# Dense expert stage: weight loads of four experts, stored first products reloaded into the lower parts' buffers

## Chip, core and metric

The kernel runs on one core of a Trainium2 chip. The time is the device time of one execution in microseconds (us). Seven names recur: PE (TensorE, the matrix engine; PEld is its weight load), DVE (VectorE), ACT (ScalarE), POOL (GpSimd), SP (the engine that issues most DMA transfers), DMA (the 16 transfer engines of the core) and PSUM (the accumulation memory that PE writes).

## What is computed

A decoder block over 1024 tokens of width 1024: two attention branches, a memory attention, and then an expert layer with 16384 experts. The change touches the expert layer alone:

```python
def peer_ffn(h, w_q, sub_keys, u, v):
    ...
    best_s, pos = lax.top_k(cand_s, PEER_TOPK)
    best_i = jnp.take_along_axis(cand_i, pos, axis=-1)
    g = jax.nn.softmax(best_s, axis=-1)
    ...
        a = jnp.einsum('cd,ced->ce', hc, u[ic])
        a = jax.nn.gelu(a, approximate=False) * gc.astype(hc.dtype)
        return jnp.einsum('ce,ced->cd', a, v[ic])
```

Each token picks 8 x 16 experts; the output is the sum over them of gelu(h . u) times a gate weight times the row v.

## The kernel before

The eight blocks of 128 tokens are treated in two ways. Blocks 0 to 3 are *gathered*: `gathered_u` (L1027) and `gathered_v` (L1041) fetch one expert row per token with an indirect DMA from POOL, 128 rows per block and table, and DVE multiplies each row (L1038 for u, L1057 for v). Seven buffers `rows` hold the fetched rows. These steps are spread over the whole program by `Pace` (L44): each piece of PE work adds its time to a budget, and a row step is written out when the budget allows, so that the written order mixes them with whatever runs. A scheduler then sets the order on each engine from priorities and its own estimate of durations; what it has set is fixed, and every engine takes its instructions strictly in that order.

Blocks 4 to 7 are *dense* (`dense`, L1190): for them all 16384 experts are computed, in 128 slices of 128 experts, with gate weights that are zero where a token has not picked the expert. Below, "expert" e stands for such a slice. For each there is a first product (h times u, 24 matmuls of 512 columns: eight column parts, each in three products of higher and lower parts), GELU, a multiplication by the gate weights, and a second product with the slice's rows of v. The helper `split` (L111) cuts a float32 tile into a higher part (ACT, L112) and a lower part (DVE, L113) for the matmuls.

Before the gate weights are complete, the first products of experts 0 to 47 are computed, passed through GELU and stored in DRAM (`ga`, L1226). From 2215 us on the second products run in groups of G = 4 experts. `group(gi)` (L1239) makes the left operands, `second(gi, cs)` (L1258) splits the four value rows and runs eight output tiles of 12 matmuls; `group(gi + 1)` is written ahead of `second(gi)`. In groups 0 to 11 a first product is reloaded from `ga` into `c` (L1248); in groups 12 to 31 `first(e)` (L1208) computes it. The buffers that matter, and what frees each:

- `wl` (2 buffers): the gate weights of two experts, 512 KB, runs of 512 bytes in DRAM; multiplied in place with the first products (L1252) and free after the split.
- `c` (1 buffer): a reloaded first product, free after L1252.
- `c0`, `c1` (7 each): higher and lower part of an expert's left operand, free when all eight tiles of the group have used them, which is at the group's end. Two groups hold eight, so the last expert of the next group waits for the first of the running one.
- `vraw` (4): a raw value row block, free after the split into `v0`, `v1` (4 each), which are again free at a group's end.
- `uraw` (3), `uT0`, `uT1` (2 each): the same for the first product.

SP issues all loads but the gathers, in one queue; an instruction that waits there holds up all that follow it.

Of the kernel before, what the change touches and what calls it, by code (L numbers as in the profile page):

```python
# [9 lines left out]
F32 = mybir.dt.float32  # L10
F32R = mybir.dt.float32r
# [3 lines left out]
AF = mybir.ActivationFunctionType  # L15
# [5 lines left out]
P = 128  # L21
# [5 lines left out]
ND = NB - NG  # L27
DT = ND * P
# [56 lines left out]
class K:  # L85
# [941 lines left out]
    def gathered_u(self, b, r):  # L1027
        nc, a, ep = self.nc, self.a, self.ep
        ii = r["ii"]
        h3 = ep.tile([P, D], F32, name="h3s", bufs=1)  # L1030
        nc.sync.dma_start(h3, self.h3[b])
        aa = r["aa"] = ep.tile([P, P], F32, name="aa", bufs=3)
        for j in range(P):
            u = self.rows()
            nc.gpsimd.indirect_dma_start(out=u, out_offset=None, in_=a["peer_u"][0],  # L1035
                                         in_offset=bass.IndirectOffsetOnAxis(ap=ii[:, j:j + 1], axis=0))
            with self.tc.issue_after(self.last_dve):
                nc.vector.scalar_tensor_tensor(u, u, 1.0, h3, op0=OP.mult, op1=OP.mult, accum_out=aa[:, j:j + 1])  # L1038
            yield self.u_each

    def gathered_v(self, b, r):  # L1041

        nc, a, ep = self.nc, self.a, self.ep
        w = ep.tile([P, P], F32, name="wexp", bufs=1)
        nc.scalar.activation(w, r["aa"], AF.Gelu)
        nc.vector.tensor_tensor(w, w, r["gg"], op=OP.mult)
        o = ep.tile([P, D], F32, name="h3s", bufs=1)
        for j in range(P):
            with self.tc.high_priority(offset=V_AHEAD):
                v = self.rows()  # L1050
                nc.gpsimd.indirect_dma_start(out=v, out_offset=None, in_=a["peer_v"][0],  # L1051
                                             in_offset=bass.IndirectOffsetOnAxis(ap=r["ii"][:, j:j + 1], axis=0))
                with self.tc.issue_after(self.last_dve):
                    if j == 0:
                        nc.vector.tensor_scalar(o, v, w[:, :1], None, op0=OP.mult)
                    else:
                        nc.vector.scalar_tensor_tensor(o, v, w[:, j:j + 1], o, op0=OP.mult, op1=OP.add)  # L1057
            yield V_EACH or self.u_each
        self.finish(b, o, [self.rows() for _ in range(3)])
        yield 1.0  # L1060
# [129 lines left out]
    def dense(self, psum, early):  # L1190

        nc, a = self.nc, self.a
# [3 lines left out]
        with ExitStack() as ctx:  # L1196
# [11 lines left out]
            def first(e):  # L1208
                uT = load_u(e)
                o = self.acc()  # L1210
                for k in range(KD):
                    self.mm3(o, [u[:, k] for u in uT], [x[:, k] for x in h3], k == 0, k == KD - 1)
                self.pace.tick(KD * 3 * 0.216)
                return o
# [20 lines left out]
            sp = E(self.pool("sp"))  # L1235
            accu = sp.tile([P, ND, D], F32, name="accu")
            G = 4

            def group(gi):  # L1239
                cs = []  # L1240
                for e in range(gi * G, gi * G + G):
                    if e % 2 == 0:
                        w2 = sp.tile([P, 2 * ND, 2, P // 2], F32, name="wl", bufs=2)
                        nc.sync.dma_start(w2, self.Wd[:, :, e:e + 2].rearrange("j p e n -> p j e n"))
                    w = w2[:, :, e % 2]
                    if e in ga:
                        c = sp.tile([P, DT], F32, name="c", bufs=1)
                        nc.sync.dma_start(c, ga[e])  # L1248
                    else:
                        c = first(e)  # L1250
                        nc.scalar.activation(c, c, AF.Gelu)
                    nc.vector.tensor_tensor(w, c.rearrange("p (j n) -> p j n", j=2 * ND), w, op=OP.mult)  # L1252
                    ch = [sp.tile([P, DT], F32R, name=f"c{j}", bufs=7) for j in range(2)]
                    self.split(w, *[x.rearrange("p (j n) -> p j n", j=2 * ND) for x in ch])
                    cs.append(ch)
                return cs

            def second(gi, cs):  # L1258
# [7 lines left out]
                for i in range(ND):  # L1266
                    for d in range(2):
# [14 lines left out]
                        self.pace.tick(G * 3 * 0.216)  # L1282

            cs = group(0)
            for gi in range(NE // G):
                nx = group(gi + 1) if gi + 1 < NE // G else None
                second(gi, cs)
                cs = nx
# [102 lines left out]
WHOLE = {("P", 1), ("G", 1), ("M", 1)}  # L1391
PAIRS = {(2, 0)}
KEEP, A_BUFS, O_BUFS = 4, 2, 2
U_BUFS, V_BUFS = 3, (4, 4, 4)
SELECT_EACH = (5.0, 7.0)
U_EACH, ROUTE_EACH = (1.9, 1.8, 1.9, 1.3, 2.0), 3.0
ROUTE_LAG, EXPERT_LAG = 300, 3000
# [31 lines left out]
```

## Time and profile before

| What | Value |
|---|---|
| median of 3 runs | 3498.06 us (3488.26 to 3505.14) |
| the profiled execution | 3498.35 us |
| its span, first to last instruction | 3496.6 us, mean granted clock 0.93 |
| PE busy | 3027.1 us (87%) |
| DVE busy | 2851.4 us (82%) |
| ACT, POOL busy | 1399.1 us (40%), 1402.9 us (40%) |
| DMA | 964.64 MB, mean 276 GB/s |

The span lies within 2 us of the profiled execution's time, and that execution within 0.3 us of the median. Busy shares are means over stages with different limits: the second products, which the change touches, fill the last 1280 us.

### The profile page before, as it was taken

How to read it: one execution, taken by the hardware profiler on the slowest of the kernel's cores; microseconds unless marked ns; L12 is line 12 of the kernel's file. 1: busy time of each engine (PE TensorE's matmuls, PEld its weight loads, DVE VectorE, ACT ScalarE, POOL GpSimd, SP SyncE). 2: the span in 40 equal slices, each digit the busy share in tenths (PEclk: the TensorE clock that was granted, in tenths of full speed). 3: DMA queues.
4: the chain of work that ended last, by engine and by line, in shares of the span. 5: the costliest groups of instructions: out<-in, count | busy, mean ns of one | idle time of the engine just before them, and what ended most of it. 6: DMA issues, size and time to landing. Idle time of an engine off the chain costs nothing. (4 is left out here: it accounts for less than half of the span.)

```text
span 3496.6 us, 42268 instructions
## 1 busy us (share of the span) xinstructions
PE 3027.1 (87%) x13234; PEld 2292.2 (66%) x13234; DVE 2851.4 (82%) x6623; ACT 1399.1 (40%) x2537; POOL 1402.9 (40%) x1122
## 2 busy tenths in 40 slices
PE   8999888798788798777998896587899999999997
PEld 6778766553345675445676674466677888787886
DVE  6656554588968989887999888687799999899998
ACT  5756344245656441323546465222122222222222
POOL 0010000012245346653122665424457666776665
PEclk9999999899898899888999998799899999999999
DMA  4575443335789579887485999989899999999998
GB/s 139 163 187 136 168 136 137 128 121 187 215 285 303 145 263 359 305 322 281 141 294 210 372 366 345 381 305 326 304 349 373 384 381 371 359 365 384 377 380 285
DMA packets 394210, 964.64 MB, mean 276 GB/s; under 512 B 36713, under 2 KB 146049, under 8 KB 392577
## 3 DMA queue, kind: packets, MB, share of 16 engines
q0 software_dynamic: 155264, 560.01, 45.1%
q1 hardware_dynamic: 238720, 401.94, 33.5%
q8 instruction: 104, 1.70, 0.2%
q14 instruction: 122, 0.99, 0.1%
HBM read 871.64 MB, written 90.18 MB: 275 GB/s over the span
## 5 line engine op out<-in xcount | busy, mean ns | idle before, releaser
L1035 POOL DMA_INDIRECT rows<-in_peer_u_dram,ii x512 | 689.0, 1346 | 916.8 <-DVE rows L1038 365.5
L1051 POOL DMA_INDIRECT rows<-in_peer_v_dram,ii x512 | 649.6, 1269 | 425.4 <-DVE h3s L1057 290.3
L1057 DVE SCALAR_TENSOR_TENSOR h3s<-rows,wexp,h3s 128x1024 f32<-128x1024 f32 x508 | 651.0, 1282 | 36.3 <-DMA rows<-in_peer_v_dram,ii 27.4
L1038 DVE SCALAR_TENSOR_TENSOR rows<-rows,h3s 128x1024 f32<-128x1024 f32 x512 | 611.6, 1219 | 79.1 <-DMA rows<-in_peer_u_dram,ii 75.7
L135 PE MATMUL acc<-fT,uT 128*128 128x512 f32 x1024 | 415.1, 405 | 43.3 <-ACT uT L112 23.9
L137 PE MATMUL acc<-fT,uT 128*128 128x512 f32 x1024 | 412.3, 403 | 13.8 <-DVE uT L113 13.7
L136 PE MATMUL acc<-fT,uT 128*128 128x512 f32 x1024 | 409.6, 400 | 0.0
L112 ACT ACTIVATE c<-wl 128x512 fp32r<-128x512 f32 x128 | 80.1, 631 | 812.2 <-PE out L136 461.6
L149 POOL TENSOR_TENSOR rstd<-msq,mhalf 128x1 f32<-128x1 f32 (+1 forms) x42 | 35.3, 840 | 592.9 <-DVE msq L147 582.5
L135 PEld LDWEIGHTS acc<-fT,uT 128*128 128x128 f32 x1024 | 196.8, 192 | 88.7 <-ACT uT L112 24.8
L137 PEld LDWEIGHTS acc<-fT,uT 128*128 128x128 f32 x1024 | 196.7, 192 | 66.5 <-DVE uT L113 20.9
L136 PE MATMUL kept<-v,c 128*128 128x512 f32 x512 | 206.7, 406 | 34.5 <-DVE v L113 34.5
L135 PE MATMUL kept<-v,c 128*128 128x512 f32 x512 | 202.3, 401 | 37.8 <-ACT v L112 36.9
L112 ACT ACTIVATE uT<-uraw 128x1024 fp32r<-128x1024 f32 x128 | 135.5, 1059 | 246.8 <-PE acc L136 130.5
L136 PEld LDWEIGHTS acc<-fT,uT 128*128 128x128 f32 x1024 | 196.9, 192 | 38.7
L113 DVE TENSOR_TENSOR w<-wraw,w 128x512 fp32r<-128x512 f32 (+1 forms) x176 | 116.8, 680 | 118.6 <-ACT w L112 112.0
L135 PE MATMUL out<-v,c 128*128 128x512 f32 x512 | 204.1, 399 | 8.9 <-DVE accu L1281 8.9
L137 PE MATMUL kept<-v,c 128*128 128x512 f32 x512 | 203.9, 398 | 0.0
L136 PE MATMUL out<-v,c 128*128 128x512 f32 x512 | 202.9, 396 | 0.0
L137 PE MATMUL out<-v,c 128*128 128x512 f32 x512 | 202.6, 396 | 0.0
L568 ACT ACTIVATE junk<-W,xb 128x384 bf16<-128x384 f32 (+5 forms) x186 | 163.7, 880 | 75.7 <-DVE xb L566 55.2
L112 ACT ACTIVATE w<-wraw 128x512 fp32r<-128x512 f32 (+1 forms) x176 | 105.9, 619 | 186.5 <-PE acc L136 81.8
(361 smaller groups left out, 6780.8 us busy)
## 6 DMA issues: line engine op xcount, KB each, us to landing
uraw<-in_peer_ut_dram SPq DMA_DIRECT2D x128, 512.0 KB
vraw<-in_peer_v_dram SPq DMA_DIRECT2D x128, 512.0 KB
Wd<-wbuf SPq DMA_DIRECT2D x64, 512.0 KB
wl<-Wd SPq DMA_DIRECT2D x64, 512.0 KB
wraw<-in_w_in_dram SPq DMA_DIRECT2D x40, 512.0 KB
fraw<-in_w_in_dram SPq DMA_DIRECT2D x32, 512.0 KB
wraw<-in_w_out_dram SPq DMA_DIRECT2D x24, 512.0 KB
ga<-gelu SPq DMA_DIRECT2D x48, 256.0 KB
```

Of the source, the lines that this page charges most:

```text
L112: self.nc.scalar.activation(hi, src, AF.Copy)
L113: self.last_dve = self.nc.vector.tensor_tensor(lo, src, hi.bitcast(F32), op=OP.subtract).ins
L135: nc.tensor.matmul(out, l[0], r[0], start=start, stop=False)
L136: nc.tensor.matmul(out, l[0], r[1], start=False, stop=False)
L137: self.last_pe = nc.tensor.matmul(out, l[1], r[0], start=False, stop=stop).ins
L149: nc.gpsimd.tensor_tensor(r, v, self.mhalf[:, :n], op=OP.pow)
L568: nc.scalar.activation(junk[:, :(b + 1) * P], self.W[b], AF.Sign, bias=xb[:, j:j + 1].bitcast(F32), accum_out=s[:, j:j + 1])
L1035: nc.gpsimd.indirect_dma_start(out=u, out_offset=None, in_=a["peer_u"][0], in_offset=bass.IndirectOffsetOnAxis(ap=ii[:, j:j + 1], axis=0))
L1038: nc.vector.scalar_tensor_tensor(u, u, 1.0, h3, op0=OP.mult, op1=OP.mult, accum_out=aa[:, j:j + 1])
L1051: nc.gpsimd.indirect_dma_start(out=v, out_offset=None, in_=a["peer_v"][0], in_offset=bass.IndirectOffsetOnAxis(ap=r["ii"][:, j:j + 1], axi ...
L1057: nc.vector.scalar_tensor_tensor(o, v, w[:, j:j + 1], o, op0=OP.mult, op1=OP.add)
```

## The change

Four edits. The gate weights of a whole group are loaded in one transfer of 1 MB (`wg`, two buffers, runs of 1024 bytes) in place of two of 512 KB. A stored first product is reloaded into the `c1` buffer of its own expert, read there as plain float32, multiplied into the weights, and the buffer then takes the lower part; the single buffer `c` is gone. `vraw` has three buffers in place of four. For the gathered blocks, `aa` has two buffers in place of three, and GELU and gate multiplication work in it in place, without `wexp`.

```diff
--- before.py
+++ after.py
@@ -1029,7 +1029,7 @@
         ii = r["ii"]
         h3 = ep.tile([P, D], F32, name="h3s", bufs=1)
         nc.sync.dma_start(h3, self.h3[b])
-        aa = r["aa"] = ep.tile([P, P], F32, name="aa", bufs=3)
+        aa = r["aa"] = ep.tile([P, P], F32, name="aa", bufs=2)
         for j in range(P):
             u = self.rows()
             nc.gpsimd.indirect_dma_start(out=u, out_offset=None, in_=a["peer_u"][0],
@@ -1041,8 +1041,8 @@
     def gathered_v(self, b, r):
 
         nc, a, ep = self.nc, self.a, self.ep
-        w = ep.tile([P, P], F32, name="wexp", bufs=1)
-        nc.scalar.activation(w, r["aa"], AF.Gelu)
+        w = r["aa"]
+        nc.scalar.activation(w, w, AF.Gelu)
         nc.vector.tensor_tensor(w, w, r["gg"], op=OP.mult)
         o = ep.tile([P, D], F32, name="h3s", bufs=1)
         for j in range(P):
@@ -1239,18 +1239,19 @@
             def group(gi):
                 cs = []
                 for e in range(gi * G, gi * G + G):
-                    if e % 2 == 0:
-                        w2 = sp.tile([P, 2 * ND, 2, P // 2], F32, name="wl", bufs=2)
-                        nc.sync.dma_start(w2, self.Wd[:, :, e:e + 2].rearrange("j p e n -> p j e n"))
-                    w = w2[:, :, e % 2]
+                    if e % G == 0:
+                        wg = sp.tile([P, 2 * ND, G, P // 2], F32, name="wl", bufs=2)
+                        nc.sync.dma_start(wg, self.Wd[:, :, e:e + G].rearrange("j p e n -> p j e n"))
+                    w = wg[:, :, e % G]
+                    ch = [sp.tile([P, DT], F32R, name=f"c{j}", bufs=7) for j in range(2)]
                     if e in ga:
-                        c = sp.tile([P, DT], F32, name="c", bufs=1)
+
+                        c = ch[1].bitcast(F32)
                         nc.sync.dma_start(c, ga[e])
                     else:
                         c = first(e)
                         nc.scalar.activation(c, c, AF.Gelu)
                     nc.vector.tensor_tensor(w, c.rearrange("p (j n) -> p j n", j=2 * ND), w, op=OP.mult)
-                    ch = [sp.tile([P, DT], F32R, name=f"c{j}", bufs=7) for j in range(2)]
                     self.split(w, *[x.rearrange("p (j n) -> p j n", j=2 * ND) for x in ch])
                     cs.append(ch)
                 return cs
@@ -1391,7 +1392,7 @@
 WHOLE = {("P", 1), ("G", 1), ("M", 1)}
 PAIRS = {(2, 0)}
 KEEP, A_BUFS, O_BUFS = 4, 2, 2
-U_BUFS, V_BUFS = 3, (4, 4, 4)
+U_BUFS, V_BUFS = 3, (4, 4, 3)
 SELECT_EACH = (5.0, 7.0)
 U_EACH, ROUTE_EACH = (1.9, 1.8, 1.9, 1.3, 2.0), 3.0
 ROUTE_LAG, EXPERT_LAG = 300, 3000
```

No arithmetic is changed. On every engine the order is the same as before up to the first weight load of the second products. Three places from there on matter. In the listings a row is one instruction: line, operation, written tile, read tile, shape; numbers behind a name tell its instances apart. In brackets stand what it waits for: PE, DVE, Activation (ACT), or the lanes of earlier transfers (DMAHW).

The first is SP's queue in the stored groups. Before, in a stretch of about one group (`wl` weights, `vraw` raw values, `c` the reloaded product):

```order
L1244 DMA wl<-Wd 128x8x128 [waits DMAHW6_49,Activation_49]
L1263 DMA vraw<-in_peer_v_dram 128x1024 [waits DMAHW7_49,DVE_49]
L1248 DMA c<-ga_15442 128x512 [waits DMAHW5_49,DVE_49]
L1263 DMA vraw<-in_peer_v_dram 128x1024 [waits DMAHW1_49,Activation_49]
L1244 DMA wl<-Wd 128x8x128 [waits DVE_49]
L1248 DMA c<-ga_15523 128x512 [waits DMAHW0_49,DVE_49]
L1263 DMA vraw<-in_peer_v_dram 128x1024 [waits DMAHW4_49]
```

After, one whole group:

```order
L1250 DMA c_19131<-ga_14748 128x512 [waits DMAHW4_49,PE_49]
L1250 DMA c_19300<-ga_14865 128x512 [waits DMAHW5_49,PE_49]
L1250 DMA c_19306<-ga_14996 128x512 [waits DMAHW6_49,PE_49]
L1250 DMA c_19312<-ga_15087 128x512 [waits PE_49]
L1264 DMA vraw<-in_peer_v_dram 128x1024 [waits DMAHW0_49,DVE_49]
L1244 DMA wl<-Wd 128x8x256 [waits DMAHW1_49,DVE_49]
L1264 DMA vraw<-in_peer_v_dram 128x1024 [waits DMAHW2_49,DVE_49]
L1264 DMA vraw<-in_peer_v_dram 128x1024 [waits DMAHW3_49,DVE_49]
L1264 DMA vraw<-in_peer_v_dram 128x1024 [waits DMAHW0_49,DMAHW4_49,DVE_49,Activation_49]
```

The reloads, which waited for DVE (L1252) one at a time, now wait for PE, four together, and the value loads stand behind them.

The second is DVE at a stored group's handover (`c_` and `v_` lower parts, `wl` the product with the weights, `accu` the sum of an output tile). Before:

```order
L113 TENSOR_TENSOR c_19933<-wl,c_19932 128x512
L113 TENSOR_TENSOR v_20130<-vraw,v_20129 128x1024
L1281 TENSOR_TENSOR accu<-accu,out 128x512
L113 TENSOR_TENSOR c_20103<-wl,c_20102 128x512
L113 TENSOR_TENSOR c_20110<-wl,c_20109 128x512
L113 TENSOR_TENSOR v_20136<-vraw,v_20135 128x1024
L1252 TENSOR_TENSOR wl<-c,wl 128x8x64
L113 TENSOR_TENSOR v_20142<-vraw,v_20141 128x1024
L113 TENSOR_TENSOR c_20119<-wl,c_20118 128x512
L113 TENSOR_TENSOR v_20148<-vraw,v_20147 128x1024
```

After:

```order
L113 TENSOR_TENSOR v_20080<-vraw,v_20079 128x1024
L1254 TENSOR_TENSOR wl<-c_19887,wl 128x8x64
L1282 TENSOR_TENSOR accu<-accu,out 128x512
L1254 TENSOR_TENSOR wl<-c_20056,wl 128x8x64
L113 TENSOR_TENSOR c_19887<-wl,c_19886 128x512
L1254 TENSOR_TENSOR wl<-c_20062,wl 128x8x64
L113 TENSOR_TENSOR c_20056<-wl,c_20055 128x512
L1254 TENSOR_TENSOR wl<-c_20068,wl 128x8x64
L113 TENSOR_TENSOR c_20062<-wl,c_20061 128x512
L113 TENSOR_TENSOR v_20086<-vraw,v_20085 128x1024
L113 TENSOR_TENSOR c_20068<-wl,c_20067 128x512
L113 TENSOR_TENSOR v_20092<-vraw,v_20091 128x1024
```

All four products of reloaded experts now stand between the first value's lower part and the second's; before, one product stood among the values and the others among the rows that follow. About ten gathered rows follow in either.

The third is DVE at a live group's handover (`h3s` a gathered row, `uT` the lower part for a first product). Before:

```order
L113 TENSOR_TENSOR c_23631<-wl,c_23630 128x512
L113 TENSOR_TENSOR v_23992<-vraw,v_23991 128x1024
L1281 TENSOR_TENSOR accu<-accu,out 128x512
L113 TENSOR_TENSOR v_23998<-vraw,v_23997 128x1024
L113 TENSOR_TENSOR v_24004<-vraw,v_24003 128x1024
L113 TENSOR_TENSOR v_24010<-vraw,v_24009 128x1024
L1057 SCALAR_TENSOR_TENSOR h3s<-rows,wexp,h3s 128x1024 x2
L1252 TENSOR_TENSOR wl<-acc,wl 128x8x64
```

After:

```order
L113 TENSOR_TENSOR c_23498<-wl,c_23497 128x512
L1282 TENSOR_TENSOR accu<-accu,out 128x512
L113 TENSOR_TENSOR v_23899<-vraw,v_23898 128x1024
L113 TENSOR_TENSOR v_23905<-vraw,v_23904 128x1024
L113 TENSOR_TENSOR v_23911<-vraw,v_23910 128x1024
L1057 SCALAR_TENSOR_TENSOR h3s<-rows,aa,h3s 128x1024 x2
L113 TENSOR_TENSOR uT_23811<-uraw,uT_23810 128x1024
L1254 TENSOR_TENSOR wl<-acc,wl 128x8x64
L113 TENSOR_TENSOR v_23917<-vraw,v_23916 128x1024
```

SP's queue beside it, before and after, one group each:

```order
L1244 DMA wl<-Wd 128x8x128
L1263 DMA vraw<-in_peer_v_dram 128x1024 x4
L1203 DMA uraw<-in_peer_ut_dram 128x1024 x2
L1244 DMA wl<-Wd 128x8x128
L1203 DMA uraw<-in_peer_ut_dram 128x1024 x2
```

```order
L1244 DMA wl<-Wd 128x8x256
L1264 DMA vraw<-in_peer_v_dram 128x1024 x3
L1203 DMA uraw<-in_peer_ut_dram 128x1024
L1264 DMA vraw<-in_peer_v_dram 128x1024
L1203 DMA uraw<-in_peer_ut_dram 128x1024 x3
```

The fourth value's lower part has moved behind a product and two gathered rows, and its raw rows, which lay in a buffer before the handover, are loaded during it, behind the weight load of 1 MB. A live group holds about 21 gathered rows in either order.

## Rows read from the trace of the kernel before

**Rows 1.** Busy time by stage: stretch, us, engines (instructions), clock, DMA share, GB/s.
```profile
core 0: us, PE busy (x) PEld busy (x) DVE busy (x) ACT busy (x) POOL busy (x), PEclk, DMA share, GB/s
2215.00:2250.00 35.00, 6.36 (x19) 4.77 (x20) 18.72 (x18) 5.37 (x6) 10.84 (x10) 0.53 1.04 395
2250.00:2400.00 150.00, 125.79 (x502) 98.48 (x501) 117.52 (x142) 37.63 (x51) 50.70 (x42) 0.92 0.94 322
...
2700.00:2900.00 200.00, 200.00 (x884) 165.54 (x883) 198.00 (x192) 54.11 (x70) 132.09 (x100) 1.00 1.02 385
2950.00:3200.00 250.00, 235.68 (x1004) 191.77 (x1002) 225.89 (x345) 65.53 (x86) 176.61 (x123) 0.97 0.98 364
```

**Rows 2.** Waits, 2210 to 2560 us: who for whom, us, times, longest.
```profile
DVE wl L1252 <- DMA c<-ga: 43.4, 25, 10.1
```

**Rows 3.** Timeline of SP, stored stage: start, us, instruction.
```profile
2257.02 0.33 SPq L1248 DMA_DIRECT2D c<-ga  x1
...
2424.58 0.32 SPq L1248 DMA_DIRECT2D c<-ga  x1
```

**Rows 4.** Timeline of DVE, stored stage; in brackets the idle time before and its end.
```profile
2263.04 0.69 DVE L1252 TENSOR_TENSOR wl<-c,wl 128x512 f32<-128x512 f32 x1 [1.74 <-DMA c<-ga]
...
2428.81 0.69 DVE L1252 TENSOR_TENSOR wl<-c,wl 128x512 f32<-128x512 f32 x1 [1.38 <-DMA c<-ga]
```

**Rows 5.** Timeline of PE, stored stage: the start, and gaps at group handovers.
```profile
2243.64 0.79 PE L135 MATMUL kept<-v,c 128*128 128x512 f32 x1 [34.10 <-ACT v L112]
...
2332.51 0.50 PE L136 MATMUL kept<-v,c 128*128 128x512 f32 x1 [3.73 <-DVE v L113]
...
2333.41 0.63 PE L136 MATMUL out<-v,c 128*128 128x512 f32 x1
...
2336.39 0.50 PE L136 MATMUL out<-v,c 128*128 128x512 f32 x1
...
2536.00 0.50 PE L136 MATMUL kept<-v,c 128*128 128x512 f32 x1 [1.36 <-DVE v L113]
```

**Rows 6.** Timeline of DVE at a live group's handover.
```profile
2775.76 0.68 DVE L113 TENSOR_TENSOR c<-wl,c 128x512 fp32r<-128x512 f32 x1
2776.36 1.22 DVE L113 TENSOR_TENSOR v<-vraw,v 128x1024 fp32r<-128x1024 f32 x1
2777.50 0.68 DVE L1281 TENSOR_TENSOR accu<-accu,out 128x512 f32<-128x512 f32 x1
2778.09 3.49 DVE L113 TENSOR_TENSOR v<-vraw,v 128x1024 fp32r<-128x1024 f32 x3
2781.50 2.60 DVE L1057 SCALAR_TENSOR_TENSOR h3s<-rows,wexp,h3s 128x1024 f32<-128x1024 f32 x2
2784.02 0.69 DVE L1252 TENSOR_TENSOR wl<-acc,wl 128x512 f32<-128x512 f32 x1
```

**Rows 7.** DMA issues: transfer, count, size of one.
```profile
vraw<-in_peer_v_dram SPq DMA_DIRECT2D x128, 512.0 KB
...
wl<-Wd SPq DMA_DIRECT2D x64, 512.0 KB
...
c<-ga SPq DMA_DIRECT2D x48, 256.0 KB
```

**Rows 8.** Timeline of SP at the same live handover.
```profile
2776.47 0.38 SPq L1244 DMA_DIRECT2D wl<-Wd  x1
2777.61 4.33 SPq L1263 DMA_DIRECT2D vraw<-in_peer_v_dram  x4
```

**Rows 9.** Timeline of ACT at the same live handover.
```profile
2773.21 3.89 ACT L112 ACTIVATE v<-vraw 128x1024 fp32r<-128x1024 f32 x4
```

**Rows 10.** Timeline of POOL at the same live handover.
```profile
2775.64 1.01 POOL L1051 DMA_INDIRECT rows<-in_peer_v_dram,ii  x1 [0.30 <-issue]
2776.96 1.43 POOL L1051 DMA_INDIRECT rows<-in_peer_v_dram,ii  x1 [0.30 <-issue]
```

**Rows 11.** Instructions on tile h3s from 2600 us: durations min/median/max, first and last start.
```profile
L1055 DVE TENSOR_SCALAR h3s<-rows,wexp x2: 753/753/753, 2695.0 to 3223.8; 128x1024 f32<-128x1024 f32 x2
L1070 DVE TENSOR_TENSOR rows<-rows,h3s x2: 1217/1222/1227, 2949.9 to 3487.9; 128x1024 f32<-128x1024 f32 x2
```

## Prediction

> **What bounds the kernel now.** I read the table by stage first. The change touches only the last third of the program, from 2215 us on, where the second products of the dense expert part run; the order of every engine before that point is unchanged. That third has two stages. In the **stored stage** (groups 0 to 11, whose first products come back from DRAM) TensorE is busy 125.8 of 150 us at a granted clock of 0.92, VectorE 117.5, and the DMA share is 0.94 [rows 1]: nobody is full, so waits in turn set the pace. In the **live stage** (groups 12 to 31, which also compute their first products) TensorE has no gap at all between 2700 and 2900 us (884 matmuls in 200 us, 0.226 us each), VectorE is busy 198 of 200, and DMA carries 385 GB/s at a share of 1.02 [rows 1]. There three resources are full together, and anything that makes VectorE stand still lengthens the kernel.
>
> The waits come second. In the stored stage VectorE stood 43.4 us for the reloaded first products [rows 2]: one buffer `c`, so each reload is asked for when the one before has been multiplied, and lands 4.2 to 6.0 us later (asked at 2424.58, used at 2428.81; asked at 2257.02, used at 2263.04) [rows 3, 4]. TensorE's gaps there end with a value's lower part from VectorE. The same gap ends at 2332.51 and, seven groups later, at 2536.00: 29.1 us a group, where 96 matmuls at 0.226 would take 21.7 [rows 5].
>
> **The change, part by part.** The profiled execution took 3498.35 us (span 3496.6); the median of the three runs is 3498.06, so the sum needs no correction.
>
> *Stored stage, the reload lands in `c1`.* Seven buffers in place of one, but a `c1` buffer is read by the matmuls until a group's last output tile. The order shows it: the reload waits for PE, four in a row at each group's end, and SP stands there with all later loads behind it. What this makes of a group, counted from its last matmul: the last tile's first expert is done nine matmuls (2.0 us) earlier, and the reload lands 4.2 us after that, at +2.2. I take the shorter of the two landings because SP has nothing else in its queue then. VectorE's order has next: product, accumulate, then product and lower part three times over; these eight take 0.60 each (as `c` and the accumulation in [rows 6]), 4.8 in all. Then comes the second value's lower part, 1.14, so it is ready at +8.2. TensorE has 15 matmuls to do before it and 81 after: 8.2 + 81 × 0.226 = 26.5. After such a gap it starts slow: from 2333.41 to 2336.39 seven starts are 0.43 apart, the lower of its two clock levels (1.2 GHz against 2.4), which cost 1.4 us [rows 5]. So 27.9 us against 29.1, and over 11 handovers **-13 us**. Bounds: with a landing of 6.0 it is 29.7 (+7 us). From below, a group cannot be shorter than its bytes: 4 × (256 + 256 + 512) KB and ten gathered rows of 512 KB, 9.4 MB at 385 GB/s, 24.5 us (-51 us) [rows 1, 7].
>
> *Its start.* Ahead of the first value row the queue held 1.31 MB (two weight loads, one reload), and now holds 3.93 (two doubled weight loads, seven reloads). TensorE stood 34.1 us until 2243.64 for that value [rows 5]; 2.62 MB more at the 395 GB/s of that stretch [rows 1] is **+6.6 us** (0 if later work catches it up, 13 at half the rate).
>
> *Live stage, three raw value buffers and one weight load of 1 MB.* Before, a group's four raw value rows lay ready at its handover, and VectorE split all four at once (2776.36 to 2781.5) [rows 6]; their reloads for the next group followed the splits [rows 8]. Now the fourth row (call it v3) is only asked for when the first is split, and on SP it stands right behind the weight load, which is asked for at the same moment as today but is twice as large. VectorE's order wants v3's lower part after c, accumulate, three values, two rows, one uT and one product. From 2775.76 that is 0.60 + 0.60 + 3.42 + 2.52 + 1.14 + 0.60 = 8.9 us, at 2784.6. When can it be there? The weight load goes at 2776.47 [rows 8]; 1.57 MB must move before v3 is complete, 4.1 us at 385 GB/s alone, 8.2 if gathered rows take half; 3.5 us of a landing is not transfer (4.2 less 0.7 for 0.26 MB); ScalarE's split takes about 1.0 (four in 3.89) [rows 9]. That makes 2785.1 to 2789.2: **VectorE stands 0.5 to 4.6 us per group**. I take 3.2, towards the shared end, because GpSimd issues gathers every 1.3 us right up to 2776.96 [rows 10], so up to seven rows are in the queues when the weights are asked for. What hides a stall is VectorE's slack, and while its products are of the V kind (gathered value rows, from 2695.0 to 2949.9 and from 3223.8 on [rows 11]) that is 2 us in 200, 0.4 a group. So 2.8 us in each of about 11 such groups: **+31 us**. In the other eight groups (U kind) VectorE already idles 24 of 250 us [rows 1], waiting for gathered rows that would land during the stall; I charge 0.6 each, **+5 us**. Bounds: low end 0.1 × 11 = 1; high end 4.2 × 11 + 2 × 8 = 62.
>
> *The rest* costs nothing I can place. The weight loads move the same bytes in half as many runs, which helps only where DMA is last. The in-place GELU is the same instruction on another tile. Two buffers for `aa` suffice, as U and V of a token block alternate. SP's long stand before weight loads in the live stage goes over to the next load.
>
> Sum: 3498.35 - 13 + 6.6 + 31 + 5 = **3528 us**. Slower; its own range is 3495 to 3575.
>
> **The rivals.** *Faster: DMA becomes the only bound of the stored stage.* For it: the 43.4 us of VectorE's waits go [rows 2], and reloads come in bursts of four. Against: the reload now stands between TensorE's last use and its next one, where it did not stand before. With groups of 24.5 us and v3 in time, 3498 - 51 + 7 + 1 = 3455 us; it decides if reloads land within about 1 us. Chance 0.16.
>
> *No change: v3 is in time.* If row gathers and weight packets take turns one by one, a load of 1024 runs of 1 KB takes no longer beside gathers than one of 1024 runs of 512 B, so v3 sees only about 0.52 MB of shared time ahead of it: 2.7 us for that, 1.4 to 2.7 for itself. It is ready at 2784.9 to 2786.2, a stall of 0.3 to 1.6, take 1.2. Then the live stage costs 0.8 × 11 = 9 and the sum is 3498 - 13 + 7 + 9 = 3501 us. The Trainium skill, page "DMA: Bandwidth & Descriptors", section on queues, rings and completion order, says that each DMA engine goes round-robin between the queues that have work, packet by packet. That is the rule by which this rival would hold; no row here shows the two queues' packets side by side. Chance 0.24.
>
> *Much slower: everything at the bad end.* Reloads of 6.0 us (+7), the start at half rate (+13), the stall at 4.6 (+62): 3580 us. It decides if gathers hold their share through the whole weight load. Chance 0.10.
>
> **How the numbers follow.** Forecast 0.50, rivals 0.16, 0.24, 0.10. About 0.5% (17 us) is what a measurement of this kernel can tell from no change. Slower by more than that, above 3516: 0.42 of the forecast's 0.50, all of the last rival, a little of the middle one, 0.54. Within: the rest of the forecast and most of the middle rival, 0.28. Faster: 0.18. The range for 8 in 10 is 3465 to 3575: it takes in the middle rival, most of the forecast's bounds, and the nearer part of both outer rivals.
>
> **What the new profile would show.** If I am right: in the stored stage one TensorE gap of 4 to 5 us per group that ends with a value's lower part, VectorE waiting once per group for a reload, groups of about 28 us, and the first value split some 6 us later than at 2243. In the live stage, ScalarE's split of every fourth value waits for its raw row, VectorE behind it, and between 2700 and 2900 us TensorE is no longer without gaps. Wrong: VectorE still 198 of 200 busy in a V stretch (no stall), or stored groups outside 25 to 30 us.

## The result, and the profile after

The change makes the kernel slower: 3627.49 us median of 4 runs against 3500.11 of the kernel before, ratio 1.038 with a 95% interval of 1.0354 to 1.0407. The forecast was 3528, the range 3465 to 3575. The profiled execution took 3621.98 us, its span is 3620.2, so 123.6 us more than before's 3496.6.

Where they lie is read from a few rows that both traces have. First VectorE's lower parts `uT` (for the live first products) after 2450 us: how many, shortest, median and longest in ns, first and last start. Before:

```profile
L113 DVE TENSOR_TENSOR uT<-uraw,uT x76: 1208/1217/1226, 2568.3 to 3426.2; 128x1024 fp32r<-128x1024 f32 x76
```

After, and then the timeline of PE at its first second product, after:

```profile
L113 DVE TENSOR_TENSOR uT<-uraw,uT x76: 1208/1216/1226, 2580.8 to 3542.7; 128x1024 fp32r<-128x1024 f32 x76
```

```profile
2249.84 0.80 PE L135 MATMUL kept<-v,c 128*128 128x512 f32 x1 [42.25 <-ACT v L112]
```

PE stood 42.25 us for its first value, 34.10 before [rows 5], so the **start** cost 8.2. From there to the first `uT`, the **stored stage** took 331.0 us, before 324.7: +6.3. From the first `uT` to the last, the **live stage** took 961.9, before 857.9: **+104.0**. From the last `uT` to the end it took 77.5, before 70.4: +7.1. The part of the program that is the same ended 1.9 us earlier in this execution. Together 8.2 + 6.3 + 104.0 + 7.1 - 1.9 = 123.7.

The stages by the columns of [rows 1], after:

```profile
2250.00:2400.00 150.00, 128.16 (x506) 99.77 (x507) 119.39 (x142) 37.48 (x48) 61.54 (x47) 0.92 0.91 319
...
2700.00:2900.00 200.00, 184.05 (x766) 149.09 (x765) 171.26 (x167) 49.20 (x65) 115.51 (x87) 0.94 0.92 329
2950.00:3200.00 250.00, 218.23 (x908) 175.95 (x907) 203.67 (x286) 60.99 (x80) 146.52 (x106) 0.92 0.92 329
```

The three resources that were full together in the live stage all have holes: in 200 us VectorE does 171.3 us of work where it did 198, TensorE 766 matmuls for 884, DMA carries 329 GB/s for 385. What VectorE stands for is in the waits from 2600 to 3400 us (who for whom, us, times, longest):

```profile
ACT v L112 <- DMA vraw<-in_peer_v_dram: 143.3, 16, 12.7
POOL rows L1051 <- DVE h3s L1057: 127.3, 45, 12.2
...
POOL rows L1035 <- DVE rows L1038: 93.1, 34, 12.1
PE acc L135 <- DVE wl L1254: 89.3, 19, 8.5
DVE v L113 <- ACT v L112: 73.1, 10, 9.5
...
DVE c L113 <- ACT c L112: 40.9, 6, 7.8
...
DVE rows L1038 <- DMA rows<-in_peer_u_dram,ii: 13.6, 12, 3.7
```

The first, fifth and sixth of these rows are not among the waits of the kernel before at all. Sixteen times ScalarE waits for a raw value row, and VectorE behind it stands 73.1 + 40.9 = 114 us, 7.1 per handover on average (where the next instruction in its order is a `c` lower part, ScalarE makes the higher part of `c` only after the late value, so the wait is put down to `c`). One handover, the one that answers to [rows 6, 8, 9]; SP, ACT and DVE:

```profile
2761.81 0.38 SPq L1244 DMA_DIRECT2D wl<-Wd  x1
2764.74 2.60 SPq L1264 DMA_DIRECT2D vraw<-in_peer_v_dram  x3
...
2961.66 0.38 SPq L1244 DMA_DIRECT2D wl<-Wd  x1
...
3224.43 0.38 SPq L1244 DMA_DIRECT2D wl<-Wd  x1
```

```profile
2775.52 1.06 ACT L112 ACTIVATE v<-vraw 128x1024 fp32r<-128x1024 f32 x1 [6.84 <-DMA vraw<-in_peer_v_dram]
2776.49 0.61 ACT L112 ACTIVATE c<-wl 128x512 fp32r<-128x512 f32 x1
```

```profile
2761.10 0.68 DVE L113 TENSOR_TENSOR c<-wl,c 128x512 fp32r<-128x512 f32 x1
...
2770.02 1.21 DVE L113 TENSOR_TENSOR uT<-uraw,uT 128x1024 fp32r<-128x1024 f32 x1
2777.14 0.69 DVE L113 TENSOR_TENSOR c<-wl,c 128x512 fp32r<-128x512 f32 x1 [5.91 <-ACT c L112]
2777.74 1.22 DVE L113 TENSOR_TENSOR v<-vraw,v 128x1024 fp32r<-128x1024 f32 x1
```

This is the stall that was forecast, at the place that was forecast: v3 is asked for when the first value is split, behind the 1 MB of weights, and is used 13.7 us after the weights were asked for (14.6 as the mean of 18 handovers, read from the same timelines). TensorE pays behind it: its next first product waits 3.80 us for VectorE's product at 2781.95. From weight load to weight load, four groups with gathered value rows take 2961.66 - 2761.81 = 199.9 us, 50.0 each, and the five groups with gathered u rows up to 3224.43 take 52.6 each. Before, from 2776.47 [rows 8] on, these were 43.4 and 48.5:

```profile
2950.02 0.38 SPq L1244 DMA_DIRECT2D wl<-Wd  x1
...
3192.52 0.38 SPq L1244 DMA_DIRECT2D wl<-Wd  x1
```

What moved between 2761.81 and 2775.52, by queue (q0 carries the gathers, q1 all of SP's loads): packets, MB, share of the 16 engines' time:

```profile
q0 software_dynamic: 825, 3.01, 58.7%
q1 hardware_dynamic: 1342, 2.18, 43.4%
```

The gathers held more than half of the engines' time throughout. And by the time v3 was there 2.18 MB of SP's loads had moved, not only the 1.57 MB of the weights and v3: what was asked for behind v3 moved beside it.

In the stored stage the signs are the forecast ones, and one more stands beside them. SP, DVE and PE, and the wait for reloads from 2210 to 2560 us, after:

```profile
2416.59 2.36 SPq L1250 DMA_DIRECT2D c<-ga  x4
```

```profile
2418.14 1.22 DVE L113 TENSOR_TENSOR v<-vraw,v 128x1024 fp32r<-128x1024 f32 x1
2423.66 0.69 DVE L1254 TENSOR_TENSOR wl<-c,wl 128x512 f32<-128x512 f32 x1 [4.30 <-DMA c<-ga]
```

```profile
DVE wl L1254 <- DMA c<-ga: 48.5, 23, 11.5
```

```profile
2314.47 0.80 PE L136 MATMUL kept<-v,c 128*128 128x512 f32 x1 [4.00 <-DVE v L113]
...
2453.96 0.50 PE L135 MATMUL out<-v,c 128*128 128x512 f32 x1 [2.08 <-DVE accu L1282]
2459.62 0.51 PE L136 MATMUL kept<-v,c 128*128 128x512 f32 x1 [3.08 <-DVE v L113]
...
2491.67 0.80 PE L136 MATMUL kept<-v,c 128*128 128x512 f32 x1 [3.33 <-DVE v L113]
```

VectorE's long wait is once per group, for the first of four reloads; the one shown was asked for at 2416.59 and used 7.1 us later, the longest of ten (4.3 to 7.1, median 5.9). In total the wait for reloads did not fall: 48.5 us, 43.4 before [rows 2]. PE stands twice per handover: first for an output tile's sum (`accu`), which VectorE makes behind the late product, then for a value's lower part. From 2314.47 to 2491.67 are six groups, 29.5 us each, against 29.1 [rows 5].

### The profile page after: what moved, and what is told of

It reads as the page before. It is cut to its first block, busy times and chain, and to the rows that moved or that the text cites. A ratio compares the mean times of both kernels' runs of the same rounds, so it can differ in the third digit from the quotient of the medians.

```text
span 3620.2 us, 42101 instructions
## 1 busy us (share of the span) xinstructions
PE 3059.6 (85%) x13234; PEld 2308.3 (64%) x13234; DVE 2855.7 (79%) x6623; ACT 1398.4 (39%) x2537; POOL 1403.1 (39%) x1122
## 4 chain that ended last, share of the span: by engine, by line
PE 33%; DVE 23%; DMA 16%; issue 15%; POOL 6%; ACT 4%; SPq 1%; POOLq 0%; ACTq 0%; DVEq 0%
DMA vraw<-in_peer_v_dram 5%; POOL rows L1035 4%; DVE h3s L1057 4%; PE acc L135 4%; PE acc L137 4%; PE acc L136 4%; DVE rows L1038 2%; PE po L727 2%; PE acc L133 2%; DMA rows<-in_peer_u_dram,ii 2%; DMA so<-pq 2%; POOL rows L1051 1%; DMA fraw<-in_w_in_dram 1%; PE kept L136 1%; PE kept L137 1%
## 5 line engine op out<-in xcount | busy, mean ns | idle before, releaser
L1051 POOL DMA_INDIRECT rows<-in_peer_v_dram,ii x512 | 657.4, 1284 | 505.8 <-DVE h3s L1057 350.7
L1057 DVE SCALAR_TENSOR_TENSOR h3s<-rows,aa,h3s 128x1024 f32<-128x1024 f32 x508 | 650.8, 1281 | 33.4 <-DMA rows<-in_peer_v_dram,ii 24.2
L135 PE MATMUL acc<-fT,uT 128*128 128x512 f32 x1024 | 429.5, 419 | 119.1 <-DVE wl L1254 95.2
L137 PE MATMUL acc<-fT,uT 128*128 128x512 f32 x1024 | 424.0, 414 | 9.9 <-DVE uT L113 9.6
L136 PE MATMUL acc<-fT,uT 128*128 128x512 f32 x1024 | 419.6, 410 | 0.0
L135 PEld LDWEIGHTS acc<-fT,uT 128*128 128x128 f32 x1024 | 204.3, 200 | 171.3 <-DVE wl L1254 105.0
L112 ACT ACTIVATE v<-vraw 128x1024 fp32r<-128x1024 f32 x128 | 128.3, 1050 | 342.6 <-DMA vraw<-in_peer_v_dram 196.2
L137 PEld LDWEIGHTS acc<-fT,uT 128*128 128x128 f32 x1024 | 202.2, 198 | 69.6 <-DVE uT L113 22.7
L136 PEld LDWEIGHTS acc<-fT,uT 128*128 128x128 f32 x1024 | 204.3, 200 | 40.9
L113 DVE TENSOR_TENSOR v<-vraw,v 128x1024 fp32r<-128x1024 f32 x128 | 152.6, 1218 | 92.4 <-ACT v L112 92.2
## 6 DMA issues: line engine op xcount, KB each, us to landing
wl<-Wd SPq DMA_DIRECT2D x32, 1024.0 KB, 11.7
```

Source lines behind the costliest of these rows:

```text
L112: self.nc.scalar.activation(hi, src, AF.Copy)
L113: self.last_dve = self.nc.vector.tensor_tensor(lo, src, hi.bitcast(F32), op=OP.subtract).ins
L135: nc.tensor.matmul(out, l[0], r[0], start=start, stop=False)
L136: nc.tensor.matmul(out, l[0], r[1], start=False, stop=False)
L137: self.last_pe = nc.tensor.matmul(out, l[1], r[0], start=False, stop=stop).ins
```

## The experiments

The first four runs put three theories against each other; each run's expectation names them. The table at the end of this section has the stages of all.

**1. Four raw rows again.** The accumulator's halves that stay in PSUM until the last group are idle SBUF; the fourth value row goes there.

```diff
+                    if e % G == G - 1:
+                        raw, vv = accu[:, :2, :512], [x.rearrange("p (j n) -> p j n", j=2) for x in vv]
+                        nc.sync.dma_start(raw, V[e * P:(e + 1) * P].rearrange("p (j n) -> p j n", j=2))
...
```

> The changed kernel, but the fourth value row of a group is loaded into 4 KB of accu that is idle until the last group, so that four raw value rows are again held; the weight load stays 1 MB and the reload stays in c1. Theory A (raw row: the live stage loses because the fourth raw row is asked for only at the handover and lands behind the 1 MB of weights): 3498 + 7 (start) - 3 (stored groups, as the profile of after has them) + 0 to 10 = 3502 to 3512 us, VectorE gap-free at the live handovers and live groups of about 43 us again. Theory B (big load: a transfer of 1 MB in one piece takes DMA from the gathered rows, whatever the raw buffers): 3600 us or more, live groups stay near 50. Theory C (the reload into c1 and the new order on SP cost the time): 3590 us or more.

Measured: 3510.05 us, ratio 1.0046 [1.0025, 1.0067]. Theory A; B and C are out. But the live stage is still 23.0 us longer than before. VectorE's wait for values is gone, and another load is late. Waits from 2600 to 3440 us:

```profile
ACT uT L112 <- DMA uraw<-in_peer_ut_dram: 65.5, 12, 9.0
```

Before, this was 6.9 us, four times. The raw rows for the first products now stand behind the 1 MB.

**2. The kernel before with three raw rows.** `V_BUFS` (4, 4, 3), nothing else.

> The kernel before with three raw value buffers in place of four, nothing else. Theory A: the fourth row is late here too, but with 0.5 MB of weights ahead of it in place of 1: about half of the stall, 3 to 4 us at each of 18 live handovers, so 3545 to 3575 us. Theories B and C: 3495 to 3505 us, since neither the 1 MB load nor the reload into c1 is there.

Measured: 3607.00 us, ratio 1.0319 [1.0289, 1.0349]. Theory A in kind, but more than it said: the one buffer, without the rest of the change, costs 73.2 us in the live stage and 32.0 in the stored one. Half the bytes ahead did not make half the stall: from 2600 to 3440 us VectorE stood 4.7 us per handover behind the late row (its waits for `v`, for `c`, and for a GELU that ScalarE does behind the late split), where it stood 7.1 in the changed kernel.

**3. The weights behind the row.**

```diff
-                        nc.sync.dma_start(wg, self.Wd[:, :, e:e + G].rearrange("j p e n -> p j e n"))
+                        with self.tc.issue_after(self.last_v if gi > 1 else self.last_load):
+                            nc.sync.dma_start(wg, self.Wd[:, :, e:e + G].rearrange("j p e n -> p j e n"))
...
```

> The changed kernel with three raw value buffers, but each weight load is put behind the fourth value row in SP's queue. Theory A: the row has nothing ahead of it and VectorE stands about 3 us per handover, as at the changed kernel's last handover, which has no weight load (3.08 us): 3498 + 4 + 18 x 2.7 + 8 (end) = about 3560, 3540 to 3575 us. Theory B: the same 1 MB goes at the same handover, 3615 to 3630 us. Theory C: 3615 to 3630 us.

Measured: 3549.95 us, ratio 1.0153 [1.0124, 1.0183], as theory A says. In the live stage 28.1 us of the 104.0 are left: what the third buffer costs with nothing ahead of the row.

**4. Weight loads of two experts and four raw rows.**

```diff
-                    if e % G == 0:
-                        wg = sp.tile([P, 2 * ND, G, P // 2], F32, name="wl", bufs=2)
+                    if e % 2 == 0:
+                        wg = sp.tile([P, 2 * ND, 2, P // 2], F32, name="wl", bufs=2)
...
-U_BUFS, V_BUFS = 3, (4, 4, 3)
+U_BUFS, V_BUFS = 3, (4, 4, 4)
```

> The changed kernel with weight loads of two experts (512 KB) and four raw value buffers: of the change only the reload into c1 and the two aa buffers are left. Theory A: 3498 + 3 (start: 2.75 MB ahead of the first value row in place of 1.31) - 3 to -10 (stored groups) = 3488 to 3500 us. Theory B: the same. Theory C: 3590 us or more.

Measured: 3509.48 us, ratio 1.0052 [1.0032, 1.0072]; above the expected 3488 to 3500, far below theory C. The live stage is before's (-0.7). The reload into `c1` does not gain in the stored stage, it costs 12.5 us there in the profiled execution.

**5 and 6. The same bytes in long runs.** Run 2 left open why 0.5 MB ahead still costs 73.2 of the 104.0 us. Both loads have 1024 runs. The loads of these two runs read one run per partition, so they leave out most of the weights; bytes and waits stay. (The expectations put the live stage's losses at 108, 85 and 34 us; by the marks of the table below they are 104.0, 73.2 and 28.1.)

```diff
-                        nc.sync.dma_start(wg, self.Wd[:, :, e:e + G].rearrange("j p e n -> p j e n"))
+                        f = (e // G) % 4 * 32
+                        nc.sync.dma_start(wg.rearrange("p j e n -> p (j e n)"),
+                                          self.Wd[0, :, f:f + 32].rearrange("p e n -> p (e n)"))
```

> The changed kernel, but each weight load of 1 MB reads one long run per partition (8 KB from the first column part alone) in place of eight runs of 1 KB, so it reads wrong weights and the output is not the reference's; instructions, waits and bytes are the same. Theory P (turns: what stands ahead of the fourth value row counts by its number of small packets, each of which waits for its turn beside 4 KB packets of gathered rows): the live stage's loss shrinks from 108 us (after) towards the 34 us of the run with the weights behind, to 40 to 60: 3545 to 3580 us in all, and the transfer of the weights takes about half as long. Theory Q (bytes, or any load ahead): 3615 to 3630 us.

> The kernel before with three raw value buffers, and each weight load of 512 KB reads one run of 4 KB per partition in place of eight runs of 512 bytes (wrong weights, so the output is not the reference's). Theory P: 128 packets in place of 1024 ahead of the fourth value row, so the live stage's loss shrinks from 85 us to 35 to 50: 3550 to 3575 us. Theory Q: 3600 to 3612 us, as with three raw buffers and short runs.

Measured: 3561.63 us, ratio 1.0200 [1.0173, 1.0227], and 3559.46, ratio 1.0177 [1.0148, 1.0206]. Both times are in theory P's range; the live stage loses 45.4 and 52.2 us (the second 2 us above what was expected of it). The landings of the weight loads between 2600 and 3440 us, min, median, max (of the 8 and 6 loads whose landing the profile tells); the changed kernel, then run 5:

```profile
L1244 SPq DMA_DIRECT2D wl<-Wd x17: 371/377/378, 2606.0 to 3428.4; - x17
...
DMA to landing us min/median/max: 11.2/12.3/16.2
```

```profile
L1245 SPq DMA_DIRECT2D wl<-Wd x18: 319/326/327, 2603.3 to 3417.9; - x18
...
DMA to landing us min/median/max: 8.2/8.6/9.1
```

The same megabyte lands 3.7 us sooner in long runs. For 0.5 MB the profile tells no landings in run 2, but v3 tells them. SP and ACT at one handover of run 2, where v3 is used 10.4 us after the weights were asked for:

```profile
2829.79 0.38 SPq L1244 DMA_DIRECT2D wl<-Wd  x1
```

```profile
2840.22 1.06 ACT L112 ACTIVATE v<-vraw 128x1024 fp32r<-128x1024 f32 x1 [8.93 <-DMA vraw<-in_peer_v_dram]
```

Read so from the timelines, as means of the 18 or 19 handovers of each run (us from asking for the weights to the use of v3; in parentheses what VectorE stood per handover):

| Ahead of v3 | 1024 short runs | one run per partition |
|---|---|---|
| 0.5 MB | 10.9 (4.7), run 2 | 10.1 (3.6), run 6 |
| 1 MB | 14.6 (7.1), the changed kernel | 11.3 (3.7), run 5 |

So long runs help at 1 MB, where they save 3.3 us, and little at 0.5 MB, where they save 0.8. The number of runs alone does not price the load: 1024 runs of 512 bytes hold v3 up 3.7 us less than 1024 runs of 1 KB. In run 5 the queues between 2745.93 (weights asked for) and 2757.06 (v3 used) moved:

```profile
q0 software_dynamic: 647, 2.34, 56.6%
q1 hardware_dynamic: 369, 1.89, 42.7%
```

The engines' time is divided between gathers and SP's loads as in the changed kernel (58.7 and 43.4%), although SP's queue finished 1342 packets to the gathers' 825 there and 369 to 647 here. One short run for one gathered row, as theory P has it, does not fit these counts.

**7. Eight c buffers.** My reading was that the stored stage gained nothing from the reload because seven `c1` buffers free the next one only at a group's end. With loads of two experts there is room for eight: `name=f"c{j}", bufs=8` on run 4's kernel.

> Weight loads of two experts, four raw value buffers, reload into c1, and eight c0 and c1 buffers in place of seven, so that two groups fit and a reload can be asked for a group ahead. My theory: the live stage as before; in the stored stage VectorE no longer waits for reloads, but TensorE still waits at each handover for the split of the first values, about 3 us and a slow restart of 1.4 us: 21.7 + 4.4 = 26 us a group against 29.2, 11 x 3 = 33 us less, so 3455 to 3475 us. Rival: the stored stage is paced by DMA and gathered rows, groups stay near 29 us: 3495 to 3510 us.

Measured: 3488.67 us, ratio 0.9979 [0.9962, 0.9995]: 4.6 us below the median of the kernel before in the same series (3493.28), where I expected 33; between theory and rival. The stored stage took 323.7 us, about before's. The 15.3 us that the profiled execution gained lie in the live stage, which I had not expected, and there in the groups with gathered u rows: 46.3 us each (weight loads at 2961.06 and, five groups on, at 3192.40) against 48.5. By the columns of [rows 1], run 7:

```profile
2950.00:3200.00 250.00, 240.24 (x1037) 194.57 (x1037) 237.03 (x363) 68.76 (x90) 173.36 (x126) 0.99 1.02 383
```

DMA carries 383 GB/s in these 250 us where it carried 364; by which step the eighth buffer does this is not shown.

**8. Five value buffers as well.** Two raw rows in the idle half of `accu`, `V_BUFS` (5, 5, ...).

> As the eight-buffer version, and besides five buffers for the split values in place of four, with two of the four raw value rows in the part of accu that is idle until the last group. My theory: the first value of the next stored group is split before the handover, so TensorE's gap per group falls by some 2 us and the group is bound by its 9.4 MB at 385 GB/s, 24.5 us: another 10 to 20 us, 3435 to 3465 us. Rival: stored groups are bound by VectorE's order or DMA already, so no difference to the eight-buffer version within 5 us.

Measured: 3476.63 us, ratio **0.9953 [0.9937, 0.9969]**, the fastest here: 12 us below run 7, short of the theory's 3435 to 3465 and more than the rival's 5 us. The stored stage takes 300.8 us, 23.9 less than before: the first value is now split ahead of the handover, and PE's wait for a lower part there is 3.3 us (ending at 2420.15) where run 7 has 5.9 (2421.32). Five value buffers without the eight c buffers were not tried.

**9 and 10. The first values first.** The first group's value rows are written ahead of the second group's loads, on run 8's and on run 1's kernel.

```diff
+                vs = values(gi) if gi == 0 else None
                 nx = group(gi + 1) if gi + 1 < NE // G else None
-                second(gi, cs)
+                second(gi, cs, vs or values(gi))
...
```

> As the version with eight c buffers and five value buffers, but the first group's value rows are written, and so asked for, ahead of the second group's weights and reloads. Theory (start: what stands ahead of the first value rows in SP's queue sets TensorE's first second product, 2251.7 there, 2243.6 before): the first product starts at 2240 to 2245, so 8 to 12 us less, 3463 to 3470 us. Rival: the second group is late in turn and takes it back within the stored stage: 3473 to 3480 us.

> The changed kernel with four raw value rows (the fourth in the idle part of accu), and the first group's value rows written ahead of the second group's weights and reloads; the weight loads stay 1 MB. Theory (the 7 us at the start come from the queue ahead of the first value row): first second product at about 2245 in place of 2251, total 3500 to 3506 us against 3510. Rival: the later stored groups set the time and it stays at 3508 to 3514 us. If this is still above the kernel before, the 1 MB load costs something even with four raw rows.

Measured: 3485.85 us, ratio 0.9955 [0.9937, 0.9974], no different from run 8 by ratio, so the rival holds in kind, though both ranges were lower. PE's idle time ahead of the first value did fall, from 42.1 to 35.8 us, but the stored stage took 11.7 more. On run 1's kernel: 3504.48, ratio 1.0026 [1.0005, 1.0046] against 1.0046, as expected, with 36.5 us of idle time for 42.3; the live stage is still 18.7 us longer than before.

**11. Without the gathered value rows.** Is a load of 1024 runs slow by itself, or beside the gathers? This kernel leaves out 15 of 16 gathers of value rows and uses each row that it has sixteen times.

```diff
-                v = self.rows()
-                nc.gpsimd.indirect_dma_start(out=v, out_offset=None, in_=a["peer_v"][0],
+                if j % 16 == 0:
+                    v = self.rows()
+                    nc.gpsimd.indirect_dma_start(out=v, out_offset=None, in_=a["peer_v"][0],
...
```

> The changed kernel, but for the second half of each gathered block only every sixteenth value row is fetched and used sixteen times, so the output is not the reference's; VectorE's and TensorE's instructions and all loads on SP's queue are as in the changed kernel. In the live stage's stretches with value rows the gathered traffic is gone, in the stretch with u rows between them it is there. Theory P (the weight load of 1024 runs is slow because each run waits its turn beside packets of gathered rows): with value rows the weights land in 5 to 7 us in place of 12.3, the fourth value row is there in time or nearly, and live groups take 43 to 44 us; with u rows landing and groups stay as in the changed kernel (12 us, 52 us). Rival Q2 (1024 runs take that long by themselves): the weights land in 10 us or more in both stretches and live groups stay near 50.

Measured (one run): 3491.79 us. SP and ACT at two handovers, the first in a stretch with value rows (gathers left out), the second with u rows (gathers there):

```profile
2735.24 0.38 SPq L1245 DMA_DIRECT2D wl<-Wd  x1
...
2965.12 0.38 SPq L1245 DMA_DIRECT2D wl<-Wd  x1
```

```profile
2742.42 1.06 ACT L112 ACTIVATE v<-vraw 128x1024 fp32r<-128x1024 f32 x1 [1.49 <-DMA vraw<-in_peer_v_dram]
...
2979.09 1.06 ACT L112 ACTIVATE v<-vraw 128x1024 fp32r<-128x1024 f32 x1 [7.50 <-DMA vraw<-in_peer_v_dram]
```

Weights and the row behind them are there 7.2 us after the weights were asked for, with gathers 14.0 (7.1 to 9.1 and 11.8 to 17.8 at the handovers of such stretches). The groups follow: from 2691.17 to 2866.14 four take 43.7 us each, and the five from 2965.12 to 3226.40 take 52.3. By the columns of [rows 1], first without gathers, then with them:

```profile
2700.00:2880.00 180.00, 180.00 (x796) 149.05 (x795) 177.08 (x172) 52.29 (x68) 0.94 (x1) 1.00 0.41 132
2930.00:3140.00 210.00, 185.52 (x768) 150.13 (x768) 177.67 (x273) 50.95 (x67) 135.64 (x95) 0.93 0.94 338
```

The rival is out: what makes the load late is what it shares the engines with. Whether the gathers cost it turns or bandwidth, this run does not tell apart.

The stages of the profiled executions in us: PE's idle time ahead of the first second product, from that to the first live `uT` (stored), to the last `uT` (live), to the end.

| Run | idle | stored | live | end |
|---|---|---|---|---|
| before | 34.1 | 324.7 | 857.9 | 70.4 |
| after | 42.3 | 331.0 | 961.9 | 77.5 |
| 1: after, 4 raw rows | 42.3 | 314.6 | 880.9 | 71.0 |
| 2: before, 3 raw rows | 34.4 | 356.7 | 931.1 | 76.9 |
| 3: after, weights behind | 42.4 | 327.9 | 886.0 | 78.4 |
| 4: after, 2 experts, 4 raw rows | 38.0 | 337.2 | 857.2 | 71.0 |
| 5: after, 1 MB in long runs | 42.0 | 326.7 | 903.3 | 77.3 |
| 6: run 2, 0.5 MB in long runs | 27.9 | 341.4 | 910.1 | 76.1 |
| 7: run 4, 8 c buffers | 42.9 | 323.7 | 842.6 | 71.0 |
| 8: run 7, 5 value buffers | 42.1 | 300.8 | 843.9 | 77.5 |
| 9: run 8, values first | 35.8 | 312.5 | 846.0 | 78.9 |
| 10: run 1, values first | 36.5 | 313.0 | 876.6 | 73.3 |
| 11: after, few value rows | 21.9 | 316.6 | 895.1 | 75.7 |

The common part ahead of these stages ended between 2196.8 and 2225.9 us in these executions (run 11, which leaves gathers out there too, apart), so a stage is compared more sharply than a whole execution. They are single executions all the same: run 1's lies 9.7 us above its median with a common part like before's, so its stages may be that much too long.

## Why the prediction was wrong

The sign of the whole, the place and the mechanism held; the size did not.

**The live stage, +31 and +5 predicted, +104.0 measured.** This is the term that failed, in two steps. First, "1.57 MB must move before v3 is complete, 4.1 us at 385 GB/s alone, 8.2 if gathered rows take half": v3 was used 13.7 us after the weights were asked for (mean 14.6), where my high end was 8.2 + 3.5 = 11.7. The gathers' half was right, and I had it only as the bad end. What I had wrong is the rest: 2.18 MB of SP's loads moved before v3 was there, and the runs of 1 KB cost 3.3 us more than long runs do (14.6 against 11.3, run 5). Run 11 shows the share of the gathers: without them 7.2 us for weights and row, and groups back at 43.7. At the handover shown, ScalarE's split of the next `c`, queued behind the late value, added 0.6. So VectorE stood 7.1 us per handover, not 3.2, above the 4.6 that I had as the worst. Second, "in the other eight groups VectorE already idles ... I charge 0.6 each": the u groups lost 4.1 us each. The slack hid 3 us of a stall and not nearly all of it: VectorE's waits for u rows only fell from 29.7 to 13.6 us. DMA was full too [rows 1], and a stall that leaves all `rows` buffers full (in these groups GpSimd stood up to 12.1 us for VectorE, 4.0 before) holds up the gathers; rows that should land during a stall are asked for late. Eleven groups at 50.0 - 43.4 = 6.6 and eight at 4.1 make 105, the loss of the stage.

**The stored stage, -13 predicted, +6.3 measured**, near my upper bound of +7. The step was "I take the shorter of the two landings because SP has nothing else in its queue then": the reload took 5.9 us (median of ten), not 4.2. That is the 6.0 of the bound, and the groups of 29.5 us are its 29.7. They also lie inside the 25 to 30 that I called right, so that sign could not tell the two apart. Run 4 shows that the reload into `c1` by itself does not gain; with eight c buffers and a fifth value buffer the stage gains 23.9 us (run 8), but which of the two does it is not separated, nor whether the reload has a part in it.

**The start, +6.6 predicted:** 8.2 more of idle time, and runs 9 and 10, which ask for the values earlier, take 6 us of it away. Right. **The end**, +7.1, was not in the sum. From the last `uT` to the first finished block both kernels need 43.4 us (3542.7 to 3586.12; before, 3426.2 to 3469.62), so a late v3 does not make it, though VectorE stands 2.55 us for one there (3577.09). The loss comes after, while the blocks are finished, where VectorE waits 3.84 us for a load of `x` (3598.37) that it did not wait for before. What delays that load is not shown.

**The rest "costs nothing"** was wrong for the weight load. With four raw rows the 1 MB still costs 18.7 to 23.0 us in the live stage (runs 10 and 1), and the u rows that stand behind it come late (65.5 us of ScalarE's waits in run 1, 6.9 before); loads of 512 KB cost nothing there (run 4).

**The rivals.** "No change" rested on this: a load of 1024 runs of 1 KB takes no longer beside gathers than one of 1024 runs of 512 bytes. It does take longer: v3 behind the first was used after 14.6 us, behind the second after 10.9 (run 2). And even with 0.5 MB ahead three raw rows cost 73.2 us, so the rival's 9 was out either way. The Trainium skill, page "DMA: Bandwidth & Descriptors", section on queues, rings and completion order, says that a DMA engine goes round-robin between queues by whole packets. The engines' time, divided 58.7 to 43.4 with short runs and 56.6 to 42.7 with long ones, fits turns of whole packets whatever the runs; where a packet ends these rows do not show. "Much slower" was the nearest rival, and its condition, that gathers hold their share through the whole load, is what happened; its 3580 us had the same price by bytes in it. "Faster" fell with the reload's landing.

What stays open: why 1 MB in short runs is 3.3 us later than in long ones beside gathers. It is not the short runs alone (run 11), and not one turn for each of them (the packet counts above). Runs 5 and 6 also read another stretch of DRAM. In the live stage the loss follows what VectorE stands per handover only in the main: 7.1, 4.7, 3.7, 3.6 and 2.5 us (the changed kernel, runs 2, 5, 6, 3) for 104.0, 73.2, 45.4, 52.2 and 28.1 us.

## What to carry to other kernels

A buffer that looks spare may be what lets a load be asked for one stage early; before one is given away, see which load then falls due at the handover and what stands ahead of it in its queue. Price a load that shares the DMA engines with gathers from a landing measured under that traffic, with loads of its own size and run length, and count what is asked for behind it as well. Where three resources are full together, idle time of one that is itself a wait for another absorbs only part of a stall.

## What the runs showed of the hardware

Beside row gathers, 1 MB in 1024 runs of 1 KB landed in 12.3 us (median), and the same 1 MB in one 8 KB run per partition in 8.6. A 512 KB row asked for behind such loads was used 14.6 and 11.3 us after them, and behind 512 KB in runs of 512 bytes and of 4 KB after 10.9 and 10.1. With the gathers left out, 1 MB in 1 KB runs and the row behind it were both there in 7.2 us. A load asked for behind others does not wait alone in line: at the handover shown 2.18 MB of SP's loads had moved by the time the row was there, where the weights and the row are 1.57 MB. The gathers held 57 to 59% of the engines' time whether SP's loads came in short or long runs.
